# Attention scores of two heads in the two row halves of TensorE, issued beside two other units' products with V

## The chip, the cores and the metric

The kernel runs on one core of a Trainium2 chip. The metric is device time in microseconds: the median of three runs, 291.02 us for the kernel before (290.55 to 291.47). One further execution was recorded by the hardware profiler; every row below is from that execution. Engines are named by their work: TensorE (PE, its weight loads PEld), VectorE (DVE), ScalarE (ACT), GpSimd (POOL), and SyncE (SP), which starts most transfers.

## The reference

One layer of a decoder block with two groups of heads: x + W_out [ HGRN2(h) * silu(g_h) ; MoBA(h) * silu(g_a) ], with h the RMS norm of x (512 x 1024). The change is in the second group, eight heads of width 64. With 512 positions and blocks of 256 keys, each query sees all keys up to its own, so it is causal attention with ALiBi:

```python
def _moba(q, k, v, q_gain, k_gain):
    q = _rms_norm(heads(q), q_gain).astype(jnp.float32)
    k = _rms_norm(heads(k), k_gain).astype(jnp.float32)
    ...
        s_own = jnp.einsum("bhqd,bhsd->bhqs", qc, k_own) * scale - slopes * dist_own
        s_own = jnp.where(dist_own >= 0, s_own, MASK_VALUE)
    ...
        p = jax.nn.softmax(s_all, axis=-1)
    ...
        return (jnp.einsum("bhqs,bhsd->bhqd", p_own, v_own)
                + jnp.einsum("bhqjs,bhqjsd->bhqd", p_sel, v_sel))
```

## The kernel before, in words

Positions lie in four tiles of 128. Most products are done in a rounded format (fp32r) with each operand split in a high and a low part, so that one f32 product becomes three: high x high, high x low, low x high. The program order of TensorE is fixed when the program is built: `drive` (L203) runs a filler, the projections one group of 512 columns after another (`fill_a`, L819) and then the first half of the output product (`out_h`, L703), and between two steps of the filler it takes a step of any thread that is ready. A thread is ready when its keys are in `done` and a latency from the table LAT (L127) has passed on a clock that counts TensorE's planned time. Every engine works its own list in order, so ScalarE's and VectorE's lists follow the same plan.

Q and K are normalised per position, turned by `qk_tr` (L522) with four transposes a tile, and evicted in two parts. Heads go in pairs p; a pair's two heads j fill 64 partitions each. Before the change each head has tiles of its own with 128 rows: for Q the high part in its own half and the low part in the other half, for K the high part in both halves, and KL the low part in both. An eviction of 64 partitions on ScalarE (L535) and one on VectorE (L536) fill the own half, transfers between partitions (L540, L542) the other one. Two products of 128 rows, Q with K and Q with KL, then make one head's scores.

Attention is cut in twelve units (L586): for each pair of heads, query tile 3, query tile 2, and tiles 1 and 0 together, with 512, 384, and 256 + 128 columns of scores. `attn_unit` (L589) is one thread per unit, started when the projections are through (L665, L880). It has three steps. First, for each head, the scores (L613, L614), on VectorE the bias and the row's extreme (L619), on ScalarE the exponential with its sum (L622), on GpSimd the division by the sum (L627). After a latency `soft` the unit's probabilities are transposed, one tile "tp" for a head, out of two buffers with the tag "tr", and copied to SBUF by ScalarE (L636). After `acopy` the products with V follow (L651), into a bank "ot" for the pair of heads; the last unit of the pair gates the result (L660 to L662), and `out_a` (L710) makes the second half of the output product from it.

The products with V and the transposes are in plain f32 and count as two instructions and one in the trace; the two heads' products with V write the lower and the upper 64 partitions of the same bank.

## Time and profile before

| | |
|---|---|
| median of three runs | 291.02 us (290.55 to 291.47) |
| the profiled execution | 290.89 us, of which 289.1 us is the span from the first to the last instruction |
| TensorE busy | 284.0 us, 98% of the span |
| VectorE, ScalarE, GpSimd busy | 174.4, 131.3, 60.4 us |
| attention on TensorE | from 212.9 to 263.6 us, with the first half of the output product between |
| granted TensorE clock, mean | 0.999 |

The chain of waits follows the work that ended last back to the start; its shares say on which engine and line the time went. A stage of the span is read by a table of windows, which gives each engine's busy time in it. In a row of the timeline the first number is the start, the second the time to the end of the row's last instruction; products are pipelined, so the time from one start to the next is what one costs. "[2.59 <-PE tp L177]" is idle time of that engine before the row, and what ended it.

### The profile page before, as it was taken

The numbers are of one execution on the slowest core, as the hardware profiler recorded it, in microseconds if no ns is written. First come the engines' busy times: TensorE is split into PE (matmuls) and PEld (weight loads), VectorE is DVE, ScalarE is ACT, GpSimd is POOL, SyncE is SP. The second block draws the span as 40 slices with busy tenths as digits, with TensorE's granted clock in tenths as the row PEclk, the third lists the DMA queues.
The fourth block names the chain that finished last, engine by engine and source line by source line (L and its number), as shares of the span: only waits on it lengthen the run. The fifth ranks groups of instructions, "written<-read, shape, count | busy, mean of one in ns | idle before, by whom it ended". The sixth has DMA issues, their size and how long they took to land.

```text
span 289.1 us, 5080 instructions
## 1 busy us (share of the span) xinstructions
PE 284.0 (98%) x1957; PEld 236.7 (82%) x1957; DVE 174.4 (60%) x371; ACT 131.3 (45%) x241; POOL 60.4 (21%) x96
## 2 busy tenths in 40 slices
PE   8899999999999999999999999999999999999995
PEld 8787888888887787898888888888888888888884
DVE  2754644744799998157855686485394577543232
ACT  3584823610610474225511843655675797652000
POOL 1006001082000000010273223420034664320000
PEclk9999999999999999999999999999999999999999
DMA  6973483340340008000620099557269000000122
GB/s 213 362 262 110 20 185 124 131 160 2 135 158 2 2 2 280 13 0 0 222 71 0 2 265 205 112 157 209 54 189 334 7 2 0 2 2 2 73 109 109
DMA packets 21386, 31.00 MB, mean 107 GB/s; under 512 B 1509, under 2 KB 8434, under 8 KB 21362
## 3 DMA queue, kind: packets, MB, share of 16 engines
q1 hardware_dynamic: 21042, 29.64, 34.7%
q0 software_dynamic: 320, 1.05, 1.0%
q8 instruction: 15, 0.25, 0.3%
q14 instruction: 9, 0.07, 0.1%
HBM read 25.17 MB, written 2.10 MB: 94 GB/s over the span
## 4 chain that ended last, share of the span: by engine, by line
PE 98%; ACT 1%; DVE 0%; issue 0%
PE acc L173 77%; PE tp L177 7%; PE sc L173 3%; PE ot L173 3%; PE pl L173 3%; PE ops L173 2%; PE wp L241 2%; PE us L173 1%; ACT whi L109 0%; ACT hTh L258 0%; DVE res L735 0%; PE tpn L245 0%; DVE nwc L246 0%; DVE scr L145 0%; PE tpv L796 0%
## 5 line engine op out<-in xcount | busy, mean ns | idle before, releaser
L173 PE MATMUL acc<-whi,hTh 128*128 128x512 f32 x160 | 64.7, 404 | 0.8 <-ACT whi L109 0.8
L173 PE MATMUL acc<-whi,hTl 128*128 128x512 f32 x160 | 62.7, 392 | 0.0
L173 PE MATMUL acc<-wlo,hTh 128*128 128x512 f32 x160 | 60.0, 391 | 0.0
L117 DVE TENSOR_TENSOR wlo<-raw,whi 128x1024 fp32r<-128x1024 f32 x39 | 47.1, 1228 | 9.2 <-ACT whi L109 8.8
L109 ACT CAST whi<-raw 128x1024 fp32r<-128x1024 f32 x40 | 41.6, 1050 | 14.3 <-DMA raw<-in_w_in_dram 6.9
L173 PE MATMUL acc<-hTh,whi 128*128 128x512 f32 x96 | 38.2, 397 | 0.0
L163 POOL TENSOR_TENSOR r<-v,mh 128x8 f32<-128x8 f32 (+1 forms) x12 | 17.2, 1431 | 99.5 <-DVE v L161 99.4
L173 PE MATMUL acc<-hTh,wlo 128*128 128x512 f32 x96 | 37.5, 391 | 0.0
L173 PE MATMUL acc<-hTl,whi 128*128 128x512 f32 x96 | 37.4, 389 | 0.0
L173 PEld LDWEIGHTS acc<-whi,hTh 128*128 128x128 f32 x160 | 30.1, 188 | 7.1 <-ACT whi L109 0.9
L173 PEld LDWEIGHTS acc<-whi,hTl 128*128 128x128 f32 x160 | 30.0, 188 | 6.7 <-DVE hTl L266 0.3
L173 PEld LDWEIGHTS acc<-wlo,hTh 128*128 128x128 f32 x160 | 30.0, 188 | 5.6
L627 POOL TENSOR_SCALAR scr<-scr,rl 128x512 f32<-128x512 f32 (+3 forms) x32 | 17.8, 568 | 17.5 <-DVE rl L625 10.2
L173 PEld LDWEIGHTS acc<-hTh,wlo 128*128 128x128 f32 x96 | 18.0, 188 | 4.0 <-DVE wlo L117 0.2
L173 PEld LDWEIGHTS acc<-hTh,whi 128*128 128x128 f32 x96 | 18.0, 188 | 3.6
L173 PEld LDWEIGHTS acc<-hTl,whi 128*128 128x128 f32 x96 | 18.1, 188 | 3.5
L699 DVE TENSOR_TENSOR res<-acc,res 128x512 f32<-128x512 f32 x15 | 10.3, 691 | 17.3 <-PE acc L173 14.6
L173 PE MATMUL acc<-whi,mTa 128*128 128x512 f32 (+1 forms) x72 | 20.4, 367 | 0.0
L622 ACT ACTIVATE scr<-scr,nm 128x512 f32<-128x512 f32 (+3 forms) x32 | 17.7, 555 | 3.1 <-DVE nm L619 1.7
L177 PE MATMUL tp<-ident,scr 128*128 128x128 f32 x128 | 18.2, 275 | 0.0
L177 PEld LDWEIGHTS tp<-ident,scr 128*128 128x128 f32 x128 | 14.9, 140 | 3.1 <-issue 0.9
L619 DVE CUSTOM_DVE_ANT_0 scr<-sc,bias 128x512 f32<-128x512 f32 (+3 forms) x32 | 14.1, 485 | 5.0 <-PE sc L173 5.0
(140 smaller groups left out, 428.1 us busy)
## 6 DMA issues: line engine op xcount, KB each, us to landing
raw<-in_w_in_dram SPq DMA_DIRECT2D x32, 512.0 KB, 4.4
raw<-in_w_out_dram SPq DMA_DIRECT2D x8, 512.0 KB, 4.4
x<-in_x_dram SPq DMA_DIRECT2D x8, 256.0 KB, 5.8
out_dram<-res SPq DMA_DIRECT2D x7, 256.0 KB, 2.1
K<-K SPq DMA_DIRECT2D x8, 128.0 KB, 5.8
KL<-KL SPq DMA_DIRECT2D x8, 128.0 KB, 6.0
Q<-scr SPq DMA_DIRECT2D x8, 128.0 KB, 2.7
res<-in_x_dram POOLq DMA_DIRECT2D x4, 256.0 KB, 7.9
```

Of the source, the lines that this page charges most:

```text
L109: nc.scalar.copy(hi, raw)
L117: eng.tensor_sub(lo, raw, hi.bitcast(F32))
L163: nc.gpsimd.tensor_tensor(r, v, mh[:, 0:n], op=ALU.pow)
L173: nc.tensor.matmul(o, a, b, start=start, stop=stop)
L177: nc.tensor.transpose(o, a, ident)
L241: nc.tensor.matmul(wp[:, 0:P], ones, ones, start=True, stop=True)
L619: nc.vector.tensor_tensor_reduce(out=z[:, o:o + n], in0=sc[:, o:o + n], in1=bias[:, j, T - n:T], op0=ALU.add, op1=ALU.min, scale=1.0, scal ...
L622: nc.scalar.activation(z[:, o:o + n], z[:, o:o + n], AF.Exp, bias=nm[:, e:e + 1], scale=-1.0, accum_out=l[:, e:e + 1])
L627: nc.gpsimd.tensor_scalar(z[:, o:o + n], z[:, o:o + n], rl[:, e:e + 1], 1.0, op0=ALU.mult, op1=ALU.mult)
L699: nc.vector.tensor_tensor(res[hf][:, u, :], ps, res[hf][:, u, :], op=ALU.add)
```

## The change

Scores use the two halves of TensorE's rows. Q and K have one high and one low tile for all heads (`A["Q"]`, `A["QL"]`, `A["K"]`, `A["KL"]`), a pair's first head in partitions 0 to 63 and its second in 64 to 127. An eviction takes all 128 partitions, and the transfers between partitions are gone. A head's scores are three products of 64 rows, and the two heads alternate, each into its own bank. The threads of the units are gone: one thread `attention`, started within the projection of V, takes two units at a time. Its step m issues the products with V of units 2m-4 and 2m-3, then the scores of 2m and 2m+1, then their gates and softmax, and after `LAT["soft"]` the transposes of 2m-2 and 2m-1, four tiles. The banks of the products with V come from the two buffers "tr", the copies go to tiles of their own, and each unit is gated by itself, into gT's own place.

```diff
...
-    LAT = dict(lm=4.544, lev0=9.2567, lev=4.4882, copy=1.9908, rms=5.7036, silu=15.1764, qk=14.2881, soft=2.5598, softn=0.0041, acopy=4.5215, st=1.5748, ch=6.6909, DEPTH=2)
+    LAT = dict(lm=4.544, lev0=9.2567, lev=4.4882, copy=1.9908, rms=5.7036, silu=15.1764, qk=14.2881, soft=1.5, two=4.0, acopy=2.6, st=1.5748, ch=6.6909)
...
@@ -526,20 +526,10 @@
             tr(tp[:, j * P:(j + 1) * P], nrm[:, j * P:(j + 1) * P])
         tpr = tp.rearrange("p (j t) -> p j t", t=P)
         ts_ = slice(u * P, (u + 1) * P)
-        low = None if key == "K" else scratch(F32R).rearrange("p (j t) -> p j t", t=P)
-        for j in range(2):
-            lo = A["KL", j][:, :, ts_] if key == "K" else low
-            own = slice(j * DH, (j + 1) * DH)
-            oth = slice((1 - j) * DH, (2 - j) * DH)
-            dst = A[key, j]
-            nc.scalar.activation(dst[own, :, ts_], tpr[own], AF.Copy, scale=gain[own])
-            nc.vector.scalar_tensor_tensor(lo[own], tpr[own], gain[own], dst[own, :, ts_].bitcast(F32),
-                                           op0=ALU.mult, op1=ALU.subtract)
-            if key == "K":
-                for z in (dst, A["KL", j]):
-                    nc.sync.dma_start(out=z[oth, :, ts_].bitcast(F32), in_=z[own, :, ts_].bitcast(F32))
-            else:
-                nc.sync.dma_start(out=dst[oth, :, ts_].bitcast(F32), in_=lo[own].bitcast(F32))
+        hi, lo = A[key], A[key + "L"]
+        nc.scalar.activation(hi[:, :, ts_], tpr, AF.Copy, scale=gain)
+        nc.vector.scalar_tensor_tensor(lo[:, :, ts_], tpr, gain, hi[:, :, ts_].bitcast(F32),
+                                       op0=ALU.mult, op1=ALU.subtract)
         done[(key, u)] = clock[0]
 
     A = {}
@@ -553,13 +543,11 @@
             if u == 0:
                 wait_for("chunks")
                 if key == "K":
-                    for j in range(2):
-                        A[key, j] = big.tile([P, NP, T], F32R, tag=tags[j], name=f"{key}{j}")
-                        A["KL", j] = big.tile([P, NP, T], F32R, tag=tags[2 + j], name=f"KL{j}")
+                    A[key], A[key + "L"] = (big.tile([P, NP, T], F32R, tag=t, name=n)
+                                            for t, n in zip(tags, (key, key + "L")))
                 else:
                     Q = big.tile([P, 2, NP, T], F32R, tag=tags[0], name=key)
-                    for j in range(2):
-                        A[key, j] = Q[:, j]
+                    A[key], A[key + "L"] = Q[:, 0], Q[:, 1]
...
@@ -581,37 +569,48 @@
         nc.scalar.activation(A["v"][:, u, :], ps, AF.Copy, scale=rst[:, u:u + 1])
         if u == 1:
             nc.scalar.activation(warm, A["v"][:, u, 0:1], AF.Exp, scale=0.0)
+            spawn(attention())
 
 
     UNITS = ((3,), (2,), (1, 0))
...
+    NU = NP * len(UNITS)
+
+    def cols_of(c):
+        p, tiles = c // len(UNITS), UNITS[c % len(UNITS)]
...
+        return p, cols, at
+
+    zs = {}
+    pts = {}
+
+    def scores(c):
+
+        p, cols, at = cols_of(c)
+        if c % len(UNITS) == 0:
+            bias = big.tile([P, 2, T], F32, tag="at", bufs=2, name="bias")
+            for j in range(2):
+                nc.gpsimd.tensor_scalar(bias[:, j, :], A["Dm"], 2.0 ** (-8.0 * (2 * p + j + 1) / AH), 1.0,
+                                        op0=ALU.mult, op1=ALU.mult)
+            A["bias"] = bias
+        bias = A["bias"]
+        scs = [psc.tile([P, 512], F32, tag="sc", name="sc") for _ in range(2)]
+        for i, o, n in cols:
+            ts_ = slice(i * P, (i + 1) * P)
+            for t, (a, b) in enumerate((("Q", "K"), ("Q", "KL"), ("QL", "K"))):
+                for j in range(2):
+                    own = slice(j * DH, (j + 1) * DH)
+                    mm(scs[j][:, o:o + n], A[a][own, p, ts_], A[b][own, p, 0:n], t == 0, t == 2,
+                       max(0.055, n / 4740.0))
+        return p, cols, at, scs, bias
+
+    def soft(c, p, cols, at, scs, bias):
+        m = len(cols)
         for j in range(2):
...
+            sc = scs[j]
...
+            zs[c, j] = z
+
+    def turn(c):
+        p, cols, at = cols_of(c)
+        m = c // 2
+        if c % 2 == 0:
+
+            pts[m] = big.tile([P, 4, 512], F32, tag=("i", "KL")[m % 2], name="pt")
         for j in range(2):
             tp = ptr.tile([P, 512], F32, tag="tr", name="tp")
+            z = zs.pop((c, j))
             for s in range(at // P):
...
+                tr(tp[:, s * P:(s + 1) * P], z[:, s * P:(s + 1) * P])
+            nc.scalar.copy(pts[m][:, 2 * (c % 2) + j, 0:at], tp[:, 0:at])
+
+    def attend(c):
+        p, cols, at = cols_of(c)
+        ot = ptr.tile([P, 512], F32, tag="tr", name="ot")
         vt = A["v"]
+        lo = min(i for i, _, _ in cols) * P
+        w = len(cols) * P
         for i, o, n in cols:
-            ts_ = slice(i * P, (i + 1) * P)
             for s in range(i + 1):
                 for j in range(2):
                     hc = slice((2 * p + j) * DH, (2 * p + j + 1) * DH)
...
+                    mm(ot[j * DH:(j + 1) * DH, i * P - lo:i * P - lo + P], vt[:, s, hc],
+                       pts[c // 2][:, 2 * (c % 2) + j, o + s * P:o + (s + 1) * P], s == 0, s == i, 0.115)
+        return p, lo, w, ot
+
+    def gate(p, lo, w, ot):
+        if "a" not in mT:
+            mTa = big.tile([P, 2, NP, T], F32R, tag="hTh", name="mTa")
+            mT["a"] = (mTa[:, 0], mTa[:, 1])
+        mTah, mTal = mT["a"]
+        mx = gT[:, p, lo:lo + w]
+        nc.vector.tensor_tensor(mx, ot[:, 0:w], mx, op=ALU.mult)
+        nc.scalar.copy(mTah[:, p, lo:lo + w], mx)
+        nc.vector.tensor_sub(mTal[:, p, lo:lo + w], mx, mTah[:, p, lo:lo + w].bitcast(F32))
+
+    def attention():
+
+        for m in range(NU // 2 + 2):
+            if m == 0:
+                yield (0.0, *[("K", u) for u in range(NT)], *[("Q", u) for u in range(NT)])
+            elif m == 1:
+                yield LAT["two"]
+            else:
+                yield (LAT["acopy"], *[(7, u) for u in range(NT)])
+            outs = [attend(c) for c in (2 * m - 4, 2 * m - 3) if m >= 2]
+            news = [(c, *scores(c)) for c in (2 * m, 2 * m + 1) if c < NU]
+            for z in outs:
+                gate(*z)
+            for z in news:
+                soft(*z)
+            if 1 <= m <= NU // 2:
+                yield LAT["soft"]
+                for c in (2 * m - 2, 2 * m - 1):
+                    turn(c)
...
-        yield from group(5, False, ev_qk("K", ("f", "k", "i", "KL"), kgs))
+        yield from group(5, False, ev_qk("K", ("f", "k"), kgs))
         yield from group(6, False, ev_qk("Q", ("q",), qgs))
         yield from group(7, False, ev_v)
 
...
-            start_attention()
             wait_for(*[("read", n) for n in range(NT)])
             yield from out_h()
```

How the lists move is shown at three places. The first is TensorE's list at the first scores; acc is a projection's bank, whi and wlo are weights. Before, they follow the first products of the output half:

```order
L173 MATMUL acc<-whi,mThh 128x512
L173 MATMUL acc<-wlo,mThh 128x512
L173 MATMUL acc<-whi,mThl 128x512
L173 MATMUL sc<-K_1554,Q 128x512
L173 MATMUL sc<-KL_1555,Q 128x512
L173 MATMUL sc<-K_1556,Q 128x512
L173 MATMUL sc<-KL_1557,Q 128x512
L173 MATMUL sc<-K_1554,Q 128x384
L173 MATMUL sc<-KL_1555,Q 128x384
L173 MATMUL sc<-K_1556,Q 128x384
L173 MATMUL sc<-KL_1557,Q 128x384
L173 MATMUL acc<-whi,mThh 128x512
```

Now they stand right behind the transposes (tp) of Q's last tile, within the projection of V:

```order
L173 MATMUL acc<-whi,hTl 128x512
L177 MATMUL tp<-ident,scr 128x128 x4
L173 MATMUL sc<-K,Q 128x512 x2
L173 MATMUL sc<-KL,Q 128x512 x2
L173 MATMUL sc<-K,Q 128x512 x2
L173 MATMUL sc<-K,Q 128x384 x2
L173 MATMUL sc<-KL,Q 128x384 x2
L173 MATMUL sc<-K,Q 128x384 x2
L173 MATMUL acc<-whi,hTh 128x512
```

The scores have moved up by the projection of V's last tiles, six instructions stand for each query tile instead of four, and nothing stands between the transposes and the products that read them.

The second place is the first turn of two units. ScalarE's list before, from the first exponentials (L622) on, with the copies of the transposes (L636):

```order
L622 ACTIVATE scr,l<-scr,nm 128x512 x2
L622 ACTIVATE scr,l<-scr,nm 128x384 x2
L636 COPY scr<-tp 128x512 x2
L622 ACTIVATE scr,l<-scr,nm 128x256
L622 ACTIVATE scr,l<-scr,nm 128x128
L622 ACTIVATE scr,l<-scr,nm 128x256
L622 ACTIVATE scr,l<-scr,nm 128x128
L636 COPY scr<-tp 128x384 x2
L622 ACTIVATE scr,l<-scr,nm 128x512 x2
L636 COPY scr<-tp 128x384 x2
```

ScalarE's list now, from the exponentials of units 2 and 3 on; the copies of units 0 and 1 are those of L640:

```order
L621 ACTIVATE scr,l<-scr,nm 128x256
L621 ACTIVATE scr,l<-scr,nm 128x128
L621 ACTIVATE scr,l<-scr,nm 128x256
L621 ACTIVATE scr,l<-scr,nm 128x128
L621 ACTIVATE scr,l<-scr,nm 128x512 x2
L109 CAST whi<-raw 128x1024 x2
L640 COPY pt<-tp 128x512 x2
L569 ACTIVATE vt<-acc,rst 128x512
L640 COPY pt<-tp 128x384 x2
```

Before, two copies come after each unit's exponentials; now four come after the exponentials of two later units and, here, two casts of weights. TensorE's list now at the same place, with the engines that an instruction waits for:

```order
L173 MATMUL acc_2090<-wlo_1890,hTh_124 128x512
L173 MATMUL acc_2090<-whi_1889,hTl_125 128x512
L177 MATMUL tp_2201<-ident_114,scr_2051 128x128 [waits PE_49,Pool_49]
L177 MATMUL tp_2201<-ident_114,scr_2051 128x128 x3
L177 MATMUL tp_2207<-ident_114,scr_2059 128x128 [waits PE_49,Pool_49]
L177 MATMUL tp_2207<-ident_114,scr_2059 128x128 x3
L177 MATMUL tp_2213<-ident_114,scr_2067 128x128 [waits Activation_49,Pool_49]
L177 MATMUL tp_2213<-ident_114,scr_2067 128x128 x2
L177 MATMUL tp_2218<-ident_114,scr_2075 128x128 [waits Activation_49,Pool_49]
L177 MATMUL tp_2218<-ident_114,scr_2075 128x128 x2
L173 MATMUL acc_2224<-whi_1901,mThh_1393 128x512
L173 MATMUL acc_2224<-wlo_1902,mThh_1393 128x512
```

The third tile of transposes (tp_2213) waits for ScalarE, the reader of the buffer's last tile.

The third place is the end of attention on TensorE, now (before, fifteen and six products of the output half stand between the last transposes and products with V):

```order
L173 MATMUL acc<-whi,mThh 128x512
L173 MATMUL acc<-wlo,mThh 128x512
L173 MATMUL acc<-whi,mThl 128x512
L177 MATMUL tp<-ident,scr 128x128 x14
L173 MATMUL ot<-pt,vt 64x128 x14
L177 MATMUL tp<-ident,scr 128x128 x12
L173 MATMUL ot<-pt,vt 64x128 x12
L173 MATMUL acc<-whi,mTa 128x512
```

Transposes and products with V of the last four units follow each other with nothing between.

## Rows read from the trace of the kernel before

**Rows 1.** The page, parts 1 (busy time by engine) and 4 (chain that ended last)
```profile
PE 284.0 (98%) x1957; PEld 236.7 (82%) x1957; DVE 174.4 (60%) x371; ACT 131.3 (45%) x241; POOL 60.4 (21%) x96
...
PE 98%; ACT 1%; DVE 0%; issue 0%
```

**Rows 2.** Table of windows: stretch, its length, each engine's busy time, clock, DMA
```profile
165.00:212.00 47.00, 47.00 (x222) 38.82 (x222) 29.42 (x41) 25.75 (x34) 9.20 (x10) 1.00 0.64 157
212.00:264.00 52.00, 52.00 (x404) 44.33 (x403) 31.06 (x107) 34.43 (x96) 22.66 (x40) 1.00 0.22 72
```

**Rows 3.** The chain in order of time: start, length, engine, tile, instructions
```profile
116.36 0.89 PE ops L173 x8
...
213.04 1.61 PE sc L173 x8
...
219.46 0.87 PE tp L177 x8
220.33 0.87 PE sc L173 x8
...
222.80 3.42 PE acc L173 x15
...
227.58 1.68 PE ot L173 x28
```

**Rows 4.** Timeline of TensorE, products behind transposes
```profile
254.64 0.47 PE L173 MATMUL acc<-whi,mThh 128*128 128x512 f32 x1
254.96 0.39 PE L173 MATMUL acc<-wlo,mThh 128*128 128x512 f32 x1
```

**Rows 5.** Timeline of TensorE, ScalarE and VectorE at Q's last tile
```profile
204.91 0.60 PE L177 MATMUL tp<-ident,scr 128*128 128x128 f32 x4
...
205.55 0.68 ACT L535 ACTIVATE Q<-tp,qgs 64x512 fp32r<-64x512 f32 x1 [1.60 <-PE tp L177]
...
206.26 0.74 DVE L536 SCALAR_TENSOR_TENSOR scr<-tp,qgs,Q 64x512 fp32r<-64x512 f32 x1 [3.04 <-ACT Q L535]
```

**Rows 6.** Groups by line and shape: evictions of 128 partitions
```profile
L517 DVE SCALAR_TENSOR_TENSOR mThl<-tp,col,mThh 128x512 fp32r<-128x512 f32 x4 | 3.0, 743 | 0.0
...
L516 ACT ACTIVATE mThh<-tp,col 128x512 fp32r<-128x512 f32 x4 | 2.7, 684 | 4.0 <-PE tp L177 4.0
```

**Rows 7.** Timeline of all engines at one unit's transposes and the next one's scores
```profile
252.24 1.09 PE L177 MATMUL tp<-ident,scr 128*128 128x128 f32 x8
252.93 1.07 ACT L636 COPY scr<-tp 128x512 f32<-128x512 f32 x2 [2.59 <-PE tp L177]
...
253.47 0.27 PE L173 MATMUL sc<-KL,Q 128*128 128x128 f32 x1
...
253.78 0.42 DVE L619 CUSTOM_DVE_ANT_0 scr<-sc,bias 128x256 f32<-128x256 f32 x1 [3.04 <-PE sc L173]
...
254.31 0.51 ACT L622 ACTIVATE scr<-scr,nm 128x256 f32<-128x256 f32 x1 [0.31 <-DVE nm L619]
```

**Rows 8.** Timeline of ScalarE: exponentials, copies, casts of weights
```profile
225.14 0.73 ACT L622 ACTIVATE scr<-scr,nm 128x512 f32<-128x512 f32 x1 [0.25 <-DVE nm L619]
...
226.58 0.86 ACT L636 COPY scr<-tp 128x384 f32<-128x384 f32 x2
228.06 0.62 ACT L622 ACTIVATE scr<-scr,nm 128x384 f32<-128x384 f32 x1 [0.62 <-DVE nm L619]
...
231.26 0.51 ACT L622 ACTIVATE scr<-scr,nm 128x256 f32<-128x256 f32 x1 [0.30 <-DVE nm L619]
...
233.03 1.04 ACT L109 CAST whi<-raw 128x1024 fp32r<-128x1024 f32 x1
233.97 0.85 ACT L636 COPY scr<-tp 128x384 f32<-128x384 f32 x2
```

**Rows 9.** Timeline of VectorE and ScalarE: a gate of 512 columns
```profile
238.32 0.68 DVE L660 TENSOR_TENSOR scr<-ot,gT 128x512 f32<-128x512 f32 x1
...
239.04 0.62 ACT L661 CAST mTa<-scr 128x512 fp32r<-128x512 f32 x1 [0.43 <-DVE scr L660]
```

More of the change, by code (lines that the diff above doesn't have):

```diff
@@ L583, in ev_v @@
             nc.scalar.activation(warm, A["v"][:, u, 0:1], AF.Exp, scale=0.0)
+            spawn(attention())
     UNITS = ((3,), (2,), (1, 0))
-    DEPTH = LAT.get("DEPTH", 2)
-    def attn_unit(c, p, tiles, ctx_):
-        need = [("K", u) for u in range(tiles[0] + 1)] + [("Q", i) for i in tiles]
-        if c >= DEPTH:
-            need.append(("sdone", c - DEPTH))
-        yield (0.0, *need)
-        if "bias" not in ctx_:
-            bias = big.tile([P, 2, T], F32, tag="at", bufs=2, name="bias")
-            for j in range(2):
-                nc.gpsimd.tensor_scalar(bias[:, j, :], A["Dm"], 2.0 ** (-8.0 * (2 * p + j + 1) / AH), 1.0,
-                                        op0=ALU.mult, op1=ALU.mult)
-            ctx_["bias"] = bias
-        bias = ctx_["bias"]
+    NU = NP * len(UNITS)
+    def cols_of(c):
+        p, tiles = c // len(UNITS), UNITS[c % len(UNITS)]
         cols = []
@@ L627, in attn_unit @@
                 nc.gpsimd.tensor_scalar(z[:, o:o + n], z[:, o:o + n], rl[:, e:e + 1], 1.0, op0=ALU.mult, op1=ALU.mult)
-            zs.append(z)
-        yield LAT["soft"] + at * LAT["softn"]
-        pts = []
+            zs[c, j] = z
[4 more added lines that the diff above has]
+            pts[m] = big.tile([P, 4, 512], F32, tag=("i", "KL")[m % 2], name="pt")
         for j in range(2):
             tp = ptr.tile([P, 512], F32, tag="tr", name="tp")
+            z = zs.pop((c, j))
             for s in range(at // P):
-                tr(tp[:, s * P:(s + 1) * P], zs[j][:, s * P:(s + 1) * P])
-            pt = scratch()
-            nc.scalar.copy(pt[:, 0:at], tp[:, 0:at])
-            pts.append(pt)
-        done[("sdone", c)] = clock[0]
-        yield (LAT["acopy"], ("sdone", c | 1), *[(7, u) for u in range(tiles[0] + 1)])
-        if "ot" not in ctx_:
-            ctx_["ot"] = psc.tile([P, 512], F32, tag="sc", name="ot")
-            ctx_["left"] = NT
-        ot = ctx_["ot"]
+                tr(tp[:, s * P:(s + 1) * P], z[:, s * P:(s + 1) * P])
[3 more added lines that the diff above has]
+        ot = ptr.tile([P, 512], F32, tag="tr", name="ot")
         vt = A["v"]
+        lo = min(i for i, _, _ in cols) * P
+        w = len(cols) * P
         for i, o, n in cols:
-            ts_ = slice(i * P, (i + 1) * P)
             for s in range(i + 1):
@@ L650, in attn_unit @@
                     hc = slice((2 * p + j) * DH, (2 * p + j + 1) * DH)
-                    mm(ot[j * DH:(j + 1) * DH, ts_], vt[:, s, hc], pts[j][:, o + s * P:o + (s + 1) * P],
-                       s == 0, s == i, 0.115)
-        ctx_["left"] -= m
-        if ctx_["left"] == 0:
-            if "a" not in mT:
-                mTa = big.tile([P, 2, NP, T], F32R, tag="hTh", name="mTa")
-                mT["a"] = (mTa[:, 0], mTa[:, 1])
-            mTah, mTal = mT["a"]
-            mx = scratch()
-            nc.vector.tensor_tensor(mx, ot, gT[:, p, :], op=ALU.mult)
-            nc.scalar.copy(mTah[:, p, :], mx)
-            nc.vector.tensor_sub(mTal[:, p, :], mx, mTah[:, p, :].bitcast(F32))
-            done[("pair", p)] = clock[0]
-    def start_attention():
-        for p in range(NP):
-            c_ = {}
-            for m, tiles in enumerate(UNITS):
-                spawn(attn_unit(p * len(UNITS) + m, p, tiles, c_))
+                    mm(ot[j * DH:(j + 1) * DH, i * P - lo:i * P - lo + P], vt[:, s, hc],
[28 more added lines that the diff above has]
+                    turn(c)
     res = {}
```

7 lines of the change are left out of this document (removed).

## The prediction

> **What bounds the kernel now.** I read the page first. TensorE is busy for 284.0 of 289.1 us, and the chain that ended last is 98% TensorE [rows 1]: time leaves this kernel only if TensorE has less to do, and any wait of TensorE adds itself in full. The table by stage says the same of the stretch that the change rewrites: from 212 to 264 us TensorE is busy for 52.00 of 52.00 us, while ScalarE has 34.43 us of work, VectorE 31.06 and GpSimd 22.66 [rows 2]. So attention is free of waits on TensorE, but it is also where ScalarE is fullest, two thirds of the time. The chain's pieces give TensorE's prices [rows 3]: eight score products of 512 and 384 columns take 1.61 us, so 0.228 for 512 and 0.175 for 384; eight of 256 and 128 take 0.87 us; a filler product of the projections takes 3.42 / 15 = 0.228; eight transposes 0.87, 0.109 each.
>
> **What the change removes.** For each pair of heads, scores need now 1.61 us for tiles 3 and 2 and 0.87 for tiles 1 and 0, of which some 0.09 is the change from transposes to products: behind transposes the second product starts 0.32 us after the first, not 0.23 [rows 4]. That is 1.61 + 0.78 = 2.39 us a pair of heads, 9.6 us in all. The new form has three products of 64 rows where two of 128 rows stood, for each head, 4 x 3 x 2 x (0.228 + 0.175 + 0.195) = 14.3 us if the two halves follow one another, half of it, 7.2, if they run side by side. No row has row halves side by side, so the change here lies between 4.7 us worse and 2.4 better. The nearest row is the one where two heads write the two halves of the output columns: a 128-column f32 instruction of 64 columns takes 1.68 / 28 = 0.060 us, while one over all columns takes 0.89 / 8 = 0.111 [rows 3]. Two halves of the columns do run together, loads included, and I take the same for the rows: -2.4 us.
> The Trainium skill, "TensorEngine Tiling (Array Packing)", section Overview, says up to twice the speed for a contraction of 64 or less; by it the term is the same. "TensorE: Matmul & The Clock Gate", Part 3, gives 3.07 times for four row tiles, not 4; an estimate from that, 14.3 / 1.54 = 9.3 us, would leave 0.3 us of gain, and no run here shows either.
>
> The 24 copies of K, KL and Q between partitions and eight of the sixteen evictions on ScalarE and on VectorE go as well. They lie beside TensorE, which never waits from 165 to 264 us [rows 2]: 0 us. Changes of form on TensorE, counted in the two orders from the first scores to the last product with V, are 23 after and 19 before, at 0.09: +0.4 us.
>
> **What the change adds: waits.** *First scores.* They now stand right behind the transposes of Q's last tile. Those begin at 204.91 and end 0.44 later; ScalarE starts to evict at 205.55 and VectorE at 206.26 [rows 5]. With all 128 partitions at once these take 0.684 and 0.743 us [rows 6]. So hi is there at 206.23, with a hand-over of about 0.15 TensorE starts at 206.38 and has waited 1.0 us; lo is there at 207.15 when the first two pairs of products (0.55) are done at 206.93, another 0.2. Before, the rest of V's projection stands between, and more: +1.2 us.
>
> *The transposes of each two units.* This is the large term. The change puts four tiles of transposes in a row where two stood, on two buffers (tag "tr", now shared with the products with V). The third tile waits until ScalarE has copied the first away, and in ScalarE's order the copies stand behind all exponentials of the next two units, whose scores TensorE has made only nine filler products before. The copies of the first and the third turn stand behind two casts of weights too. TensorE works in order, so nothing passes the waiting transpose.
> I count from the start of the scores, S. TensorE comes to the third tile after the scores (three pairs of products: 1.27 us for units (1,0)+(3), 1.11 for (2)+(1,0), 1.21 for (3)+(2)), two changes of form, nine fillers (2.05) and two tiles of transposes (0.87 or 0.66): S + 4.4, 4.0, 4.1, 4.4 and 4.0 in the five turns that scores precede.
> ScalarE: from the last score product of a bank to VectorE's start some 0.2, from there to the exponential 0.53 [rows 7]. Exponentials take 1.77 us for both heads of (1,0) (231.26 to 233.03), 1.44 for a pair of 512 columns (225.14 to 226.58), 1.22 for two of 384 at 0.61; a cast takes 0.94 (233.03 to 233.97), a copy 0.43 for 384 columns [rows 8] and 0.54 for 512 [rows 7].
> - Turn 1: first exponential at S + 1.17, 3.21 of exponentials, 1.88 of casts, copy 0.54, hand-over 0.15: S + 6.95, a wait of 2.6 us.
> - Turns 2 to 5 have two gates ahead of the softmax on VectorE. A gate goes VectorE, ScalarE, VectorE; 512 columns wide the first step takes 0.72 and the cast 0.62 [rows 9]. At 128 and 256 columns I estimate 0.9 and 1.3 for the three; the second of them ends 1.1 to 1.5 us after S. So first exponentials at S + 1.7, 2.25, 2.05 and 1.7.
> - Turn 2: 1.7 + 2.99 + 0.43 + 0.15 = 5.27, wait 1.3. Turn 3, with two casts: 2.25 + 2.66 + 1.88 + 0.58 = 7.37, wait 3.3. Turn 4: 2.05 + 3.21 + 0.69 = 5.95, wait 1.6. Turn 5 as turn 2: 1.3.
> Sum 10.1; the fourth tile waits about 0.1 each time: +10.6 us. Bounds: if ScalarE were free, a copy would begin 0.69 us after eight transposes began [rows 7], and the third tile would still wait 0.5 (0.69 + 0.54 + 0.15 against 0.87) and the fourth 0.15, 3.2 us in five turns; a third more than my sum is 14.
>
> *The end.* The fillers run out with the last scores. Then come 14 transposes, 14 products with V, 12 and 12 on two buffers, with nothing between. Four hand-overs of up to 0.8 us (0.25 + 0.4 copy + 0.15), covered in part by the other buffer: +1.6 us (0.5 to 3). The output products behind them begin with three pairs of heads, nine products for each of two tiles, 4.1 us of cover for the last gates.
>
> **Sum.** -2.4 + 0.4 + 1.2 + 10.6 + 1.6 = +11.4 us on the profiled execution's 290.89, which is 289.1 of span and 1.8 around it and lies 0.13 under the median: 302.3 us.
>
> **Rivals.**
> - *Halves in turn.* If the 64-row products do not overlap, scores cost 7.2 us more, but TensorE then comes later to every third tile, by 0.6 to 1.1 us net in each turn, so some 4.7 of waits go: about +13.9, 304.8 us. For it: no row of row halves. Against: the column halves [rows 3]. It is the change not doing what it says.
> - *ScalarE has room.* If the exponentials are done before the transposes come, each turn costs 0.65, the sum is -2.4 + 0.4 + 1.2 + 3.2 + 1.6 = +4.0, 294.9 us. For it: two thirds is not full [rows 2]. Against: the copies' place in the queue.
> - *Faster.* TensorE never waits in the turns, nor at the end, and only the work counts: -2.4 + 0.4 = -2.0, 288.9 us. This decides if all waits together stay under 2 us. For it: no wait of that kind in 212 to 264 us now [rows 2]. Against: there two tiles go to two buffers, and other work follows each time [rows 3].
> - *The clock falls.* The granted clock is 1.00, the level of 2.4 GHz, through attention [rows 2], and no row shows it after a wait of 2 to 3 us. At 1.2 GHz each product of 0.228 would take twice that; if 2 us were lost in that way behind each of the two longest waits it would be 306, behind all five 312 us. The Trainium skill, "TensorE: Matmul & The Clock Gate", Part 4, says that transposes do not count as activity for the clock as products do, and here the long waits lie between transposes; by that rule this rival would come true. The trace now has eight transposes in a row at the full level [rows 3], followed at once by products.
>
> **Chances.** The forecast with its own spread (295.4 to 307: the waits of the turns from 4.8, half as much again as their lower bound, to 14, the end from 0.5 to 3) 0.68; halves in turn, 305 and with longer waits up to 309, 0.12; ScalarE has room 0.06; faster 0.08; the clock 0.06. The range, 294.5 to 309, takes in the first three and leaves out the last two. A measurement of this kernel can tell about 0.3% from no change, 0.9 us. Faster 0.09, same 0.03, slower 0.88.
>
> **What would show it.** TensorE's waits on the copies of L640, five of 1 to 3.5 us each and the longest in turns 1 and 3; a wait of 1 us ahead of the first scores; 14 transposes that take over 3 us; scores of some 7.2 us in the chain, 9.6 now; no TensorE idle time outside attention. I am wrong if the copies come at once behind the transposes, or if the waits add up to under 5 us.

## The result, and the profile after

The changed kernel takes 307.12 us (306.1 to 308.46) where the kernel before takes 291.07 us on the same chip: a ratio of 1.054 (1.052 to 1.057), 16.05 us slower. The forecast was 302.3 us, in a range from 294.5 to 309. Its profiled execution has a span of 306.0 us, before 289.1.

The page after, parts 1 and 4, to be held against [rows 1]:

```profile
PE 288.8 (94%) x1989; PEld 237.2 (78%) x1989; DVE 170.5 (56%) x379; ACT 127.1 (42%) x241; POOL 61.3 (20%) x96
...
PE 85%; ACT 8%; DVE 4%; issue 2%; POOL 0%; ACTq 0%; DVEq 0%
```

Before, 98% of the chain was TensorE; now 12% is ScalarE and VectorE. Where that lies is told by the waits of TensorE from 200 us on (what waited, for what; us in total, how often, the longest):

```profile
PE tp L177 <- ACT pt L640: 9.3, 5, 3.4
PE tp L177 <- POOL scr L626: 1.2, 1, 1.2
PE sc L173 <- ACT Q L530: 0.8, 1, 0.8
PE tp L177 <- DVE gT L662: 0.4, 1, 0.4
PE ot L173 <- ACT pt L640: 0.2, 1, 0.2
```

One by one they stand in the timeline of TensorE: the first scores, and in each of the five turns the third tile of transposes (of turn 1 also the two tiles ahead of it):

```profile
206.94 0.50 PE L173 MATMUL sc<-K,Q 64*128 64x512 f32 x2 [0.78 <-ACT Q L530]
...
217.45 1.03 PE L177 MATMUL tp<-ident,scr 128*128 128x128 f32 x8
221.85 1.51 PE L177 MATMUL tp<-ident,scr 128*128 128x128 f32 x6 [3.37 <-ACT pt L640]
...
234.83 1.06 PE L177 MATMUL tp<-ident,scr 128*128 128x128 f32 x8 [1.27 <-ACT pt L640]
...
248.20 1.08 PE L177 MATMUL tp<-ident,scr 128*128 128x128 f32 x6 [2.85 <-ACT pt L640]
...
261.52 1.00 PE L177 MATMUL tp<-ident,scr 128*128 128x128 f32 x6 [1.20 <-POOL scr L626]
...
273.43 1.06 PE L177 MATMUL tp<-ident,scr 128*128 128x128 f32 x8 [1.51 <-ACT pt L640]
```

The wait that is put down to GpSimd is ScalarE's too: in the row below, the first of turn 4's two copies starts at 260.81 and ends a little past the middle of the row's 1.04 us, some 0.15 ahead of TensorE's start at 261.52, while GpSimd works on the next units' divisions.

```profile
260.81 1.04 ACT L640 COPY pt<-tp 128x512 f32<-128x512 f32 x2
```

There is a second loss. The table of windows (stretch, length, busy time of PE, PEld, DVE, ACT, POOL, granted clock, DMA share, GB/s) around turns 1 and 3:

```profile
212.00:218.00 6.00, 6.00 (x41) 4.62 (x40) 4.73 (x15) 4.11 (x12) 1.84 (x4) 1.00 0.33 98
218.00:221.00 3.00, 0.48 (x5) 0.24 (x3) 1.21 (x6) 3.00 (x6) 2.90 (x7) 1.00 0.94 260
221.00:225.00 4.00, 3.15 (x11) 2.79 (x12) 1.73 (x2) 2.72 (x6) 3.80 (x5) 0.57 0.85 270
225.00:228.00 3.00, 3.00 (x21) 2.25 (x21) 0.69 (x1) 0.00 (x0) 0.00 (x0) 1.00 1.00 296
...
248.00:252.00 4.00, 3.80 (x13) 3.16 (x14) 1.13 (x1) 1.39 (x4) 0.00 (x0) 0.60 0.00 0
```

Behind the two longest waits the granted clock is at 0.5, its lower level of 1.2 GHz, for some 3 us (0.57 and 0.60 are means of 4 us); behind the other three it is 1.00.

For all kernels of this study I add up TensorE's timeline by kind of work, from the transposes of Q's last tile (204.91 before, 205.57 after) to the first output product that reads attention (263.61 and 280.41): the time from each row's start to the next row's, less the idle time shown. That takes in what follows the start of a row, and leaves out where the execution began, which differs by up to 1.5 us.

| us | transposes | fillers | scores | products with V | idle | all |
|---|---|---|---|---|---|---|
| before | 8.4 | 29.7 | 10.9 | 9.6 | 0.0 | 58.7 |
| after | 11.5 | 32.8 | 9.1 | 9.6 | 11.9 | 74.8 |

The difference, 16.1 us, is that of the medians. The spans of these two executions differ by 16.9, of which 0.7 lies ahead of the stretch (204.91 against 205.57).

### The profile page after: what moved, and what is told of

It is laid out like the page before. It is cut to its first block, busy times and chain, and to the rows that moved or that the text cites. A ratio compares the mean times of both kernels' runs of the same rounds, so it can differ in the third digit from the quotient of the medians.

```text
span 306.0 us, 5085 instructions
## 1 busy us (share of the span) xinstructions
PE 288.8 (94%) x1989; PEld 237.2 (78%) x1989; DVE 170.5 (56%) x379; ACT 127.1 (42%) x241; POOL 61.3 (20%) x96
## 4 chain that ended last, share of the span: by engine, by line
PE 85%; ACT 8%; DVE 4%; issue 2%; POOL 0%; ACTq 0%; DVEq 0%
PE acc L173 69%; PE tp L177 6%; ACT scr L621 4%; PE pl L173 3%; PE ot L173 2%; PE ops L173 2%; ACT whi L109 2%; PE wp L241 2%; DVE scr L618 1%; ACT pt L640 1%; PE us L173 1%; ACT mTa L663 1%; DVE gT L662 1%; DVE mTa L664 1%; PE sc L173 1%
## 5 line engine op out<-in xcount | busy, mean ns | idle before, releaser
L117 DVE TENSOR_TENSOR wlo<-raw,whi 128x1024 fp32r<-128x1024 f32 x39 | 46.8, 1228 | 11.6 <-ACT whi L109 11.3
L177 PE MATMUL tp<-ident,scr 128*128 128x128 f32 x128 | 19.3, 283 | 10.9 <-ACT pt L640 9.3
L714 DVE TENSOR_TENSOR res<-acc,res 128x512 f32<-128x512 f32 x15 | 10.3, 692 | 30.4 <-PE acc L173 30.4
L173 PEld LDWEIGHTS acc<-whi,mTa 128*128 128x128 f32 x72 | 13.1, 189 | 2.4 <-issue 0.2
```

The source lines that it names most:

```text
L117: eng.tensor_sub(lo, raw, hi.bitcast(F32))
L173: nc.tensor.matmul(o, a, b, start=start, stop=stop)
L177: nc.tensor.transpose(o, a, ident)
L714: nc.vector.tensor_tensor(res[hf][:, u, :], ps, res[hf][:, u, :], op=ALU.add)
```

## The experiments

All changes are against the changed kernel, if nothing else is said. The kernels of the table, in the same sums:

| us | transposes | fillers | scores | with V | idle | all | median, ratio to before (95%) |
|---|---|---|---|---|---|---|---|
| halves_old_order | 10.6 | 30.5 | 9.7 | 9.6 | 0.2 | 60.5 | 293.34, 1.0062 (1.0043 to 1.0081) |
| full_row_between | 10.3 | 30.4 | 11.4 | 9.6 | 0.0 | 61.8 | 294.31, 1.0089 (1.0071 to 1.0107) |
| old_scores_new_order | 11.1 | 29.7 | 10.6 | 9.6 | 8.2 | 69.3 | 303.38, 1.0414 (1.0372 to 1.0456) |
| head_after_head | 11.6 | 31.3 | 9.5 | 9.6 | 12.4 | 74.4 | 307.74, 1.0556 (1.0529 to 1.0584) |
| casts_behind | 11.0 | 31.9 | 9.1 | 9.6 | 8.5 | 70.1 | 302.90, 1.0395 (1.0372 to 1.0419) |
| copies_first | 11.0 | 30.3 | 9.1 | 9.6 | 6.6 | 66.6 | 299.94, 1.0301 (1.0259 to 1.0344) |
| turns_split | 8.8 | 31.6 | 8.7 | 9.6 | 2.8 | 61.6 | 294.27, 1.0090 (1.0066 to 1.0114) |
| turns_split_old_scores | 8.4 | 30.7 | 10.5 | 9.7 | 0.9 | 60.2 | 293.46, 1.0058 (1.0037 to 1.0080) |
| turns_split_2 | 8.5 | 31.4 | 8.7 | 9.6 | 0.0 | 58.3 | 291.40, 1.0004 (0.9984 to 1.0024) |
| turns_split_2_old_scores | 8.5 | 30.8 | 10.5 | 9.6 | 0.0 | 59.4 | 292.39, 1.0039 (1.0023 to 1.0055) |

### The halves alone

In the kernel before, only tiles, evictions and score products are changed:

```diff
+        scs = [psc.tile([P, 512], F32, tag="sc", name="sc") for _ in range(2)]
...
+            for t, (a, b) in enumerate((("Q", "K"), ("Q", "KL"), ("QL", "K"))):
+                for j in range(2):
+                    own = slice(j * DH, (j + 1) * DH)
+                    mm(scs[j][:, o:o + n], A[a][own, p, ts_], A[b][own, p, 0:n], t == 0, t == 2, us)
```

> The kernel before with the row-half scores alone: whole tiles of Q, QL, K and KL, three products of 64 rows for each head, the two heads' products in turn on two banks; threads, order and everything else of the kernel before. My theory: the two halves run side by side, scores take 7.2 us instead of 9.6 and TensorE still does not wait, so 291.1 - 2.4 = 288.7 us (288.2 to 289.5). Rival, the halves follow one another: 14.3 us of scores, 295.8 us. Rival, the new tiles or evictions bring a wait of their own: over 290 us, with a wait of TensorE in K's or Q's stage or ahead of the first scores.

None of the three: 293.34 us, 0.6% slower, with 0.18 us of waits. The first scores in its timeline:

```profile
213.58 0.39 PE L173 MATMUL acc<-whi,mThl 128*128 128x512 f32 x1
213.89 0.50 PE L173 MATMUL sc<-K,Q 64*128 64x512 f32 x2
214.23 0.40 PE L173 MATMUL sc<-KL,Q 64*128 64x512 f32 x2
214.46 0.57 PE L173 MATMUL sc<-K,Q 64*128 64x512 f32 x4
...
215.05 0.34 PE L173 MATMUL sc<-K,Q 64*128 64x384 f32 x2
215.32 0.50 PE L173 MATMUL acc<-whi,mThh 128*128 128x512 f32 x1
215.66 0.39 PE L173 MATMUL acc<-wlo,mThh 128*128 128x512 f32 x1
```

The halves do run side by side: a pair of 512 columns takes 214.46 - 214.23 = 0.23 us, as one product of 128 rows did. But the last product ahead of them takes 0.31 instead of 0.23 and the first pair 0.34, and on the way out the last pair of 384 takes 0.27 instead of 0.18 and the first product 0.34: 0.2 us to go in and 0.2 to come out. Twelve units in the old order pay it twelve times. The sums tell the same: scores 1.2 us less, transposes (which stand ahead of most units) 2.1 and fillers 0.7 more. The Trainium skill, "TensorEngine Tiling (Array Packing)", section Tiling Modes, says that a change of the tiling mode drains TensorE, and gives no price. This trace is in line with it, with 0.2 us each way; the prediction passed that sentence over.

To measure one passage by itself, a full-row product was put into four of the units:

```diff
+            if i == 0:
+                nc.tensor.matmul(scs[0][:, 384:512], A["Q"][:, p, ts_], A["K"][:, p, 0:P], start=True, stop=True)
```

> The kernel of halves_old_order (293.3 us) with one more product of 128 rows and 128 columns, into columns that nothing reads, between the two tiles of each of the four units (1,0), so that TensorE goes from 64 rows to 128 and back once more in each. My theory, formed after halves_old_order: each pass from 128-row work into 64-row work and back costs about 0.38 us beside the products (0.18 in, 0.2 out), so the four cost 4 x (0.06 + 0.38) = 1.8 us and it takes 295.1 us; in the timeline the unit's products take 0.44 more. Rival, the row halves are slow for another reason (their loads, their banks) and the pass costs no more than the 0.09 of a change of form: 4 x 0.15 to 0.2 = 0.6 to 0.8 us, 294.0 us.

```profile
220.90 0.29 PE L173 MATMUL sc<-K,Q 64*128 64x256 f32 x2
221.12 0.33 PE L601 MATMUL sc<-K,Q 128*128 128x128 f32 x1
221.37 0.33 PE L173 MATMUL sc<-K,Q 64*128 64x128 f32 x2
```

Scores take 1.77 us more, 0.44 for each product. An extra product of 128 columns is itself 0.06 to 0.11, so out and in again costs some 0.35. The median moved less, by 0.27% or 0.8 us, since 0.4 us of transposes and wait went elsewhere; its interval reaches to 1.5. By itself the median would fit the rival of 0.6 to 0.8 us; it is the rows that decide.

### The order alone, and the order of the heads

```diff
-            for t, (a, b) in enumerate((("Q", "K"), ("Q", "KL"), ("QL", "K"))):
-                for j in range(2):
...
+            for j in range(2):
+                for t, b in enumerate(("K", "KL")):
+                    mm(scs[j][:, o:o + n], A["Q"][:, p, ts_], A[b][:, p, 0:n], t == 0, t == 1,
...
```

> The changed kernel with two products of 128 rows for each head and bank, as many and as wide as before, in the place of the six of 64 rows; its order on TensorE is the changed one. Left out is the separation of the two heads in the scores: each product sums over both heads. My theory: the whole loss comes from the order, so the waits of the turns stay (each about 0.2 us shorter, since TensorE comes later to the third tile) and 2.4 us of scores come back: 307.1 + 2.4 - 1.0 = 308.5 us (307.5 to 309.5), clock falls behind turns 1 and 3 as in the changed kernel. Rival, the row halves themselves make the waits (the last bank is ready later, or the change of form costs more than 0.09): under 303 us.

The forecast of 308.5 us missed. The whole loss is not the order's: without the halves it is 12 us, not 16. Scores and fillers tell what the halves are worth in this order: scores take 10.6 - 9.1 = 1.5 us less, although 0.2 of theirs is a wait for QL, and the fillers, apart from the clock, 0.6 more: 1.5 + 0.2 - 0.6 = 1.1 us gained. But 3.7 us of waits came with them, and between these two executions 2.9 us of lower clock (below). The clock's share is not shown to be the halves': the execution recorded here, 301.73 us, is the shortest of its four and has the clock at 1.00 all through the stretch, while the other three, 302.94 to 305.63 us, have a mean granted clock of 0.983 to 0.994, so it fell there too. Part of the waits is VectorE's list. In turn 2 of the changed kernel both heads' banks are ready late, and the list has the last step of the second gate ahead of the softmax:

```profile
230.16 0.29 DVE L664 TENSOR_TENSOR mTa<-gT,mTa 128x128 fp32r<-128x128 f32 x1 [0.37 <-ACT mTa L663]
230.37 0.55 DVE L618 CUSTOM_DVE_ANT_0 scr<-sc,bias 128x384 f32<-128x384 f32 x1
```

With one head after the other and full rows the first bank is ready earlier, and the softmax goes first:

```profile
227.76 0.56 DVE L617 CUSTOM_DVE_ANT_0 scr<-sc,bias 128x384 f32<-128x384 f32 x1
228.25 0.28 DVE L663 TENSOR_TENSOR mTa<-gT,mTa 128x128 fp32r<-128x128 f32 x1
```

Counted from the first score (229.19 and 227.11) the softmax starts after 1.18 and 0.65 us, and the turn's wait is 1.27 there and 0.35 here.

```diff
-            for t, (a, b) in enumerate((("Q", "K"), ("Q", "KL"), ("QL", "K"))):
-                for j in range(2):
+            for j in range(2):
+                for t, (a, b) in enumerate((("Q", "K"), ("Q", "KL"), ("QL", "K"))):
```

> The changed kernel with the three products of the first head in a row and then those of the second, in the place of the two heads in turn. If the halves run side by side only where neighbours use different rows, as I think, a 512-column product of 64 rows starts 0.23 us after the one before it, scores take 7.2 us more, TensorE comes 0.6 to 1.1 us later to each third tile, and the first head's bank is ready earlier, so that 4 to 6 us of the waits go: 308 to 310 us. If the engine finds the overlap in any order, the products start 0.11 us apart on average and only the earlier bank counts: 304 to 307 us.

The time, 307.74 us, lies between the two forecasts and cannot tell; the timeline can. The overlap is found in either order: the scores ahead of turn 1 take 215.11 - 213.52 = 1.59 us in this timeline, against 215.27 - 213.69 = 1.58 with the heads in turn.

```profile
206.33 0.50 PE L173 MATMUL sc<-K,Q 64*128 64x512 f32 x1 [0.78 <-ACT Q L530]
206.67 0.39 PE L173 MATMUL sc<-KL,Q 64*128 64x512 f32 x1
207.12 0.66 PE L173 MATMUL sc<-K,Q 64*128 64x512 f32 x3
...
213.52 0.39 PE L173 MATMUL sc<-K,Q 64*128 64x256 f32 x2
...
215.11 0.50 PE L173 MATMUL acc<-whi,hTh 128*128 128x512 f32 x1
```

The first three rows are the first scores, where QL comes late. There the new order shows: two products of the first head start alone, and the second head's only at 207.12, behind the one that waits for QL. The first of them takes 206.67 - 206.33 = 0.34 us alone, as a pair does in the same place of the changed kernel (206.94 to 207.28). So a product of 64 rows is not by itself half as long as one of 128; the gain is two of them at once.

### What the third tile waits for

Only TensorE's list is fixed by the program; the other engines' lists are sorted when the program is built, and `issue_after` queues what it holds behind one instruction of the same engine. Here it queues four splits of weights behind a turn's last copy:

```diff
+        if 36 <= n < len(stream) and not now:
+            late.append(n)
...
+                with tc.issue_after(last.ins):
+                    while late:
+                        split(late.pop(0), True)
```

> The changed kernel; the four last splits of weights, which nothing needs before the last output products, are held back and queued on ScalarE behind the copies of the turn that follows. My theory: the waits of turns 1 and 3 are ScalarE's queue, and two casts (1.88 us) stand in each: 3.37 becomes 1.5 to 2.1 (the copy of V's tile now stands ahead of turn 1's copies) and 2.85 becomes 1.0; the clock stays at 1.00 behind waits that short; 307.1 - 1.5 - 1.9 - 3.5 = 300.2 us. Rival, the lower clock does not come from the length of the wait: the waits fall and the granted clock still drops to 0.5, 303.7 us. Rival, the third tile waits for something else than the casts: 307 us.

Turn 3 waits 0.95 instead of 2.85, turn 1 2.05 instead of 3.37: in the changed kernel the casts are in ScalarE's queue ahead of the copies, as said. (The rows name GpSimd; the copies that free the buffer end some 0.1 to 0.2 us ahead of them.)

```profile
220.19 1.09 PE L181 MATMUL tp<-ident,scr 128*128 128x128 f32 x6 [2.05 <-POOL scr L630]
...
244.95 0.89 PE L181 MATMUL tp<-ident,scr 128*128 128x128 f32 x6 [0.95 <-POOL scr L630]
```

But the clock fell behind the 2.05 us all the same, which costs 1.6 us of fillers, most of the difference between 302.9 and the 300.2 forecast:

```profile
217.00:220.00 3.00, 1.14 (x10) 0.81 (x8) 1.17 (x7) 3.00 (x11) 2.84 (x7) 1.00 0.86 237
...
221.00:224.00 3.00, 3.00 (x9) 2.41 (x8) 1.24 (x2) 2.59 (x4) 2.25 (x4) 0.50 1.04 369
```

In the next kernel it queues the softmax there (TensorE's list is unchanged):

```diff
+            if not first and news:
+                with tc.issue_after(last.ins):
+                    for z in news:
+                        soft(*z)
```

> The changed kernel with the same order on TensorE; on ScalarE the exponentials of turns 1 to 4 (not of the last) are queued behind the copies of the turn instead of ahead of them, which also brings the casts ahead of the exponentials. My theory: the third tile waits for the first copy's place in ScalarE's queue and for nothing else, so turns 1 to 4 wait the lower bound of 0.5 and 0.15 instead of 3.37, 1.27, 2.85 and 1.20 us, the clock stays at 1.00, turn 5 keeps its 1.5: 307.1 - 8.7 + 2.6 - 3.5 = 297.5 us. Rival, ScalarE has too much to do in any order: the later exponentials make the probabilities late and the first tile of the next turn waits in place of the third, over 302 us. Rival, the third tile waits for VectorE or GpSimd: no change, 307 us.

Turns 2 and 4 wait 0.33 us, for a lower bound of 0.5; turn 3 waits 0.95 and turn 1 1.76, since there the first copy stands behind a cast of weights that came late itself. In turn 1:

```profile
219.40 1.04 ACT L109 CAST whi<-raw 128x1024 fp32r<-128x1024 f32 x1 [1.24 <-PE tp L177]
220.35 1.07 ACT L640 COPY pt<-tp 128x512 f32<-128x512 f32 x2
```

The clock is at 1.00 throughout this execution. In the sums 5.3 us of idle time and the 2.9 of the clock are gone; the median, 299.94 us for the 297.5 forecast, is 7.2 us lower than the changed kernel's. One of the four times is 302.08 us, with a mean granted clock of 0.989: there it fell.

### The clock

The waits of turns 1 and 3 were filled with work that nothing reads, once with products (the edit below), once with transposes:

```diff
+        if c in (1, 5):
+            d = psc.tile([P, 512], F32, tag="sc", name="d")
...
+            for _ in range(12):
+                nc.tensor.matmul(d, A["K"][:, 0, 0:P], A["K"][:, 0, :], start=True, stop=True)
```

> The changed kernel with 12 products of 512 columns, into a bank that nothing reads, ahead of the third tile's transposes of turns 1 and 3, where TensorE waited 3.37 and 2.85 us: 12 x 0.228 = 2.74 us of the wait is filled, nothing else changes. My theory: the waits end when ScalarE has copied, filled or not, and the lower clock behind them comes from TensorE's having been idle; filled, the granted clock stays at 1.00 and the 3.5 us that transposes and products lost at 0.50 come back: 307.1 - 3.5 = 303.6 us. Rival, the lower clock comes from something else (the transposes themselves, the row halves): granted clock 0.50 behind turns 1 and 3 as before, 307 us.

> As fill_products, with 25 transposes (25 x 0.109 = 2.7 us) of a tile that has been transposed already in the place of the 12 products. By the page of the Trainium skill "TensorE: Matmul & The Clock Gate", Part 4, transposes do not count as products do, and the granted clock would fall behind turns 1 and 3 as in the changed kernel: 307 us. If the engine's being busy is all that counts, it stays at 1.00: 303.6 us.

fill_products takes 305.09 us, 1.0456 (1.0438 to 1.0473), and fill_transposes 305.74, 1.0473 (1.0451 to 1.0495). Turn 1's third tile starts 14.91 us behind the first scores in the changed kernel and in fill_products alike, turn 3's 7.27 and 7.28 us behind the scores before it: the waits are as long, filled or not. With products the granted clock is 1.00 in every stretch, and 2.6 us come back (1.0544 - 1.0456 of 291). My 3.5 us were read too high: from the starts, the 15 fillers behind turns 1 and 3 take 4.50 and 5.14 us in the changed kernel and 3.60 and 3.63 in old_scores_new_order, and transposes 0.5 more, 2.9 us together. With transposes in the wait it stays at 1.00 at both turns as well (turn 1 below), and in the recorded execution falls later, at the end:

```profile
217.00:222.00 5.00, 4.39 (x39) 3.95 (x38) 3.20 (x7) 5.00 (x12) 4.86 (x8) 1.00 0.98 288
222.00:226.00 4.00, 4.00 (x24) 3.10 (x24) 0.89 (x2) 0.98 (x3) 2.32 (x4) 1.00 0.90 241
...
272.00:274.00 2.00, 2.00 (x22) 2.00 (x20) 0.76 (x2) 0.40 (x1) 0.00 (x0) 0.50 0.00 0
```

So idle time, not the transposes, is what the clock fell for at turns 1 and 3, and the rule of the Trainium skill, "TensorE: Matmul & The Clock Gate", Part 4, that transposes do not count as products do, does not show at the two places where it was tried. The trace lists these transposes as products with the identity; whether they are the kind that the page means, no run here shows. Whether the rule has to do with the fall at the end, behind transposes and a wait of 1.53 us, is open. Nor does a wait's length alone decide: the clock fell behind waits of 3.37, 2.85, 2.62 (head_after_head, turn 3) and 2.05 us, and not behind 3.16, 3.11, 2.46 and 2.16 us in head_after_head and old_scores_new_order.

Nor does the kernel. The changed kernel's recorded execution has two falls and a mean granted clock of 0.989 over the whole span. Four of its six executions have that mean and take 307.02 to 308.46 us; two have 0.994, one fall by the same measure, and take 306.10 and 306.36. fill_products has 0.998 or more in all four: the changed kernel never goes without a fall, and the filled one never has one. fill_transposes has 1.000 in two (305.00 and 305.61 us) and 0.994 and 0.992 in two, so in half of its executions the clock fell nowhere in the stretch.

### An order without waits

The same work, with V's fillers ahead of the first scores, fillers between the two halves of each turn, and ScalarE's copies ahead of its exponentials:

```diff
-                yield LAT["soft"]
-                for c in (2 * m - 2, 2 * m - 1):
-                    turn(c)
+                if m < 5:
+                    yield 0.6
+                turn(2 * m - 2)
+                yield (0.6 if m == 6 else 1.2)
+                last = turn(2 * m - 1)
+                with tc.issue_after(last.ins):
+                    for z in news:
+                        ex = soft(*z)
```

> The changed kernel's scores, tiles and pairs of units, as many products of every kind, in another order: two steps of V's projection ahead of the first scores; the transposes of a turn's first unit, two steps of filler, those of the second; the copies ahead of the exponentials in ScalarE's queue (the first of the last two units excepted); the four last splits of weights behind exponentials; two steps of filler kept for the end. My theory, from the starts of TensorE's instructions between Q's last transposes and the first output product: the kernel before needs 58.7 us there without a wait; this order needs 57.3 (transposes 8.5, scores 8.8, V's products 9.6, fillers 29.7 and 0.6 for coming out of the row halves), so without waits 291.1 - 1.4 = 289.7 us, and I allow 1 us of waits: 290.5 us (289.5 to 292). Rival, ScalarE has too much to do for any such order: waits of more than 4 us and over 294 us.

Missed: 294.27 us. 2.8 us of waits are left, 1.9 of them in turn 5. In ScalarE's timeline there, two exponentials stand between the first copy and the second, and wait for VectorE, which has two subtractions for weights ahead of them:

```profile
254.27 0.48 ACT L645 COPY pt<-tp 128x384 f32<-128x384 f32 x1 [0.29 <-PE tp L181]
256.50 0.61 ACT L625 ACTIVATE scr<-scr,nm 128x384 f32<-128x384 f32 x1 [1.75 <-DVE nm L622]
257.11 0.60 ACT L625 ACTIVATE scr<-scr,nm 128x384 f32<-128x384 f32 x1
257.71 0.94 ACT L645 COPY pt<-tp 128x384 f32<-128x384 f32 x2
```

> As turns_split, with two products of 128 rows for each head and bank in the place of the three of 64 rows (left out, as in old_scores_new_order: the separation of the two heads in the scores). My theory, formed after halves_old_order: six passes into the row halves and back cost most of what the shorter products save, so this is 1.1 to 1.3 us slower than turns_split and no more. Rival, the forecast's term: 2.4 us slower, less 0.4.

Missed: by the medians it is 0.3% faster, though the intervals overlap. In turn 5 its ScalarE list came out with both copies together, and its waits are 0.9 us in all. The waits hide what was asked. With the three waits mended, both kernels have none (two of the three edits):

```diff
+            if m == 7:
+                with tc.issue_after(cast.ins):
+                    while late:
+                        split(late.pop(0), True)
...
-            if m == 5:
-                soft(*news.pop(0))
```

> turns_split with its three waits mended: all exponentials of the last pair queued behind the copies too, the two last splits of weights behind the last gate (their subtractions on VectorE stood ahead of the last softmax), one step of filler more ahead of turn 2. My theory: the 2.81 us of waits and 0.2 us of lost run-up at each of the three go, and TensorE needs 61.6 - 2.8 - 0.6 = 58.2 us between Q's last transposes and the first output product, where the kernel before needs 58.7: about 0.5 us faster than before, 291 us (290 to 292), which a measurement may not tell from no change. Rival, other waits come in their place: over 293 us.

> turns_split_2 with two products of 128 rows for each head and bank (left out: the separation of the two heads in the scores). My theory: with no wait in either, this is slower than turns_split_2 by what six passes leave of the row halves' gain, 1.1 to 1.3 us in old_scores_new_order and the changed kernel: 292.2 us. Rival, the halves gain nothing where nothing waits: within 0.5 us of turns_split_2.

The table of windows of turns_split_2, against [rows 2]:

```profile
212.00:264.00 52.00, 51.99 (x433) 42.22 (x432) 30.06 (x111) 33.47 (x96) 20.32 (x38) 1.00 0.22 72
```

As forecast: 58.3 us for 58.7, the same time as before within some 0.2%, and the halves are worth 1.1 us in the sums (1.8 of scores less 0.7 of fillers) and 0.35%, 1.0 us, in the medians (the intervals just touch). So the row halves gain a little where two units share a passage and nothing waits; the passages, and the extra changes between transposes and fillers that the split turns make (with the old scores too, 30.8 us of fillers for 29.7), eat most of it. No version beats the kernel before by more than can be measured.

## Why the prediction was right in its sign and where its terms failed

Term by term, what was forecast and what the changed kernel's trace has:

| us | forecast | measured |
|---|---|---|
| scores and changes of form | -2.0 | -1.4 |
| first scores | +1.2 | +1.2 |
| third and fourth tiles of five turns | +10.6 | +11.8 |
| the end | +1.6 | +1.6 |
| lower clock behind turns 1 and 3 | 0 | +2.9 |
| sum | +11.4 | +16.1 |

The sign, the place of the waits and their cause were right. The forecast was 4.8 us too low, and 307.1 lies at the upper end of its own spread (295.4 to 307). That it is well inside the range of 294.5 to 309 is luck: the top was put there for the halves in turn, which did not happen, and what filled it was a lower clock for which the sum had no term.

- **The waits of the turns** came where and why they were forecast, with 2.6, 1.3, 3.3, 1.6 and 1.3 for 3.37, 1.27, 2.85, 1.20 and 1.51. copies_first and casts_behind show that it is the place of the copy in ScalarE's list. Turn 1 was too small because "first exponential at S + 1.17" left out VectorE, which had two subtractions of weights ahead of the softmax, as its timeline shows; the exponential came at 216.07, S + 2.38. And each wait costs some 0.2 us more than its row of idle time: eight transposes take 1.03 us to their end (217.45, above) where it is 0.80 to the next start (219.29 to 220.09 in the kernel before). That is 1.2 us in five turns; 0.4 more lies in the rows of the third and fourth tiles, for which the forecast had 0.5. With both, 10.2 us of idle time are 11.8.

```profile
213.27 2.36 DVE L117 TENSOR_TENSOR wlo<-raw,whi 128x1024 fp32r<-128x1024 f32 x2 [1.35 <-ACT whi L109]
215.55 0.42 DVE L618 CUSTOM_DVE_ANT_0 scr<-sc,bias 128x256 f32<-128x256 f32 x1
```

- **The first scores**, 0.78 + 0.22 for QL + 0.24 of the same kind, and **the end**, 0.9 of idle time and 0.7 in the transposes, were right.
- **The scores.** Side by side was right, by the row of the column halves, and so was -2.4 for the products. "Changes of form, 23 after and 19 before, at 0.09" is the step that failed here, a small one in this order: passing into row halves and out again costs twice 0.2, six times in this order, twelve in the old one, where it eats the whole gain. The rival of halves in turn is out.
- **The clock** was a rival with a chance of 0.06 and came true at the two places named, with 2.9 us for the 4 of that rival. The reason given for it, the transposes, is not what the fills show: it was the idle time. Of the 4.7 us by which the change cost more than forecast, the clock is 2.9, the turns are 1.2, the scores 0.6. The rival's time was 306, and it is 307.1.
- ScalarE has room, and faster: out, though turns_split_2 shows that ScalarE's 33 us of work in 52 do fit if its list has the copies first and the turns are split.

## What to carry to other kernels

Before a change of order, write down for each buffer the place of its reader in that engine's own list, not its load: an engine two thirds full made TensorE wait 10 us in the turns. With the copies ahead of the exponentials (copies_first) 5 of these were gone, and all of them once the turns were split and the weights' casts moved as well. Row halves must save more than some 0.4 us each time TensorE enters and leaves them, so group them. A wait of TensorE of some 2 us can cost another 1.3 to 1.6 us in clock, in one execution and not in the next, so price both and look at more than one execution.

## What the runs showed that was not expected

- Going into 64-row products and back took 0.35 to 0.4 us.
- TensorE overlaps the two halves also when three products of one head precede those of the other (1.59 and 1.58 us), while one 64-row product alone takes as long as a pair (0.34 us in the same place).
- The granted clock fell to 0.5 for about 3 us behind waits of 1.53 to 3.37 us in some places, and stayed at 1.00 behind waits of up to 3.16 us in others, and the same kernel has a different number of falls in different executions; what tells them apart is open.
